# The copies of each pair's k, and the loads of a gain row, issued by GpSimd in an attention and gMLP kernel

## The chip, the core and the metric

One core of one Trainium2 chip runs the whole program. The metric is device time in microseconds of one execution. TensorE (PE) multiplies and transposes, VectorE (DVE) and ScalarE (ACT) do elementwise work, GpSimd (POOL) does a few memsets and copies, and SyncE (SP) issues most DMA transfers. Each engine takes its instructions in order. When an instruction must wait, all that stands behind it on the same engine waits too, and that holds for an engine that only issues DMAs.

## The reference

`x` is 512 by 1024 in float32. Two layers run one after the other, each with a mixer and a squared-ReLU MLP behind it. The first mixer is chunked attention with 16 heads of 64 columns, the second a gated MLP. Cut to the parts that matter here:

```python
def chunked_relpos_attention(h, w_in, q_gain, k_gain, rel_bias, w_out):
    q, k, v = jnp.split(h @ w_in, 3, axis=-1)
    q = rms_norm(q.reshape(B, S, A_HEADS, A_HEAD_DIM), q_gain) * (A_HEAD_DIM ** -0.5)
    k = rms_norm(k.reshape(B, S, A_HEADS, A_HEAD_DIM), k_gain)
    ...
        s = jnp.einsum('bihd,bjhd->bhij', qc, kb).astype(jnp.float32) + bias
        ...
        p = jax.nn.softmax(s, axis=-1).astype(vb.dtype)
        return jnp.einsum('bhij,bjhd->bihd', p, vb)
    ...
    return o @ w_out

def chunked_spatial_gating(h, w_in, v_gain, w_s, b_s, w_out):
    z = jax.nn.gelu(h @ w_in, approximate=False)
    u, v = jnp.split(z, 2, axis=-1)
    v = rms_norm(v, v_gain).reshape(B, nw, SG_WINDOW, SG_GROUPS, SG_HALF // SG_GROUPS)
    ...
    return (u * vm.reshape(B, S, SG_HALF)) @ w_out

def reference(x, c, ...):
    cond = jax.nn.silu(c)
    for i in range(DEPTH):
        mod = cond @ ada_w[i] + ada_b[i]
        sh1, sc1, g1, sh2, sc2, g2 = [t[:, None, :] for t in jnp.split(mod, 6, axis=-1)]
        h = rms_norm(x, norm_mix[i]) * (1.0 + sc1) + sh1
        ...
        x = x + g1 * y
        h = rms_norm(x, norm_ffn[i]) * (1.0 + sc2) + sh2
        x = x + g2 * squared_relu_mlp(h, ffn_w1[i], ffn_w2[i])
    return x
```

## The kernel before

Every product of two float32 matrices is made of parts in a shorter format: an operand is split into a rounded part ("hi") and what is left ("lo"), and products of the parts are added up in one bank of PSUM. So each weight block passes through three steps: a DMA loads it (L385 for blocks of k by 512 columns, L400 for the slabs of the attention's input weights), ACT casts it to hi (L388, L405), and DVE makes lo (L389, L406). SBUF is cut into 49 slots of 4 KB per partition (`SL`, tiles named `s`), PSUM into 8 banks (`PS`, tiles named `p`). A slot or bank is taken by the next tile that asks, and that tile's first writer waits for the last reader of the one before. A DMA into a used slot so waits for whoever read the old contents, copies by DMA among them.

The attention runs by pairs of heads, 0 to 7, in software-pipelined steps:

- `pair_a` (L1141) makes q and k of a pair from normed tokens: PE transposes them (L1149), q is split (L1153 on ACT, L1154 on DVE), and k is scaled and split into one buffer `kp`, hi by L1158 on ACT and lo by L1159 on DVE. Each head has 64 of the 128 partitions of `kp`. Eight DMA copies (L1163) per pair, SBUF to SBUF, 64 partitions by 512 columns (128 KB) each, put each head's k onto both halves of the partitions: hi into `ka`, lo into `kb`. With q hi on one half and q lo on the other, one matmul with `ka` and one with `kb` give all the products of a score block.
- `head_a` (L1171) loads a head's bias (L1177 on SP) and masks a corner of it (a memset on GpSimd, L1178).
- `head_b` (L1183) makes scores row block by row block: two matmuls (the helper's line, L92) with `ka` and then `kb`, bias and maximum on DVE (L1200), exp on ACT (L1205). Behind the second head of a pair, GpSimd widens the reciprocal row sums (L1210).
- `head_c` transposes the probabilities (L1238) and splits them (L1242 on ACT, L1243 on DVE). `head_d` multiplies them with v (L92), takes the result out of its bank (L1266 on ACT, L1267 on DVE), and scales by the row sums (L1273, L1275, L1282, L1283).

Between these steps stand fillers: the remaining projections of q, k and v (`filler`, with L400, L405, L406), reads of the conditioning weights (L179, L194), and towards the end the loads of the output weights `a_w_out` (`out_load`, L385) and of x again (L115).

In the gMLP, `u_block` (L1528) runs over six column blocks. Each loads a row of gains, spread over 128 partitions (`gain`, 256 KB, one buffer, L1531), which DVE uses at L1543. The gated half v was stored to DRAM by GpSimd before (L1410) and is read back by SP (L1415).

The order of instructions on every engine comes from a scheduler that works with its own estimates of durations, so an edit at one place can move instructions of other engines. SP's DMAs take turns on eight semaphores, GpSimd's on eight of their own; an issue waits for the DMA eight issues before it on the same ring.

Of the kernel before, what the change touches and what calls it, by code (L numbers as in the profile page):

```python
# [52 lines left out]
def trunk_kernel(  # L53
# [20 lines left out]
    V, A, G, T, SP = nc.vector, nc.scalar, nc.gpsimd, nc.tensor, nc.sync  # L74
# [10 lines left out]
    def f32(ap):  # L85
        return ap.bitcast(F32)

    def bank():
        return PS.get([P, 512], F32)
# [4 lines left out]
    def mm3(ps, lh, ll, rh, rl, start, stop, more=False):  # L94

        mm(ps, lh, rh, start, False, more)
        mm(ps, lh, rl, False, False, more)
        mm(ps, ll, rh, False, stop, more)
# [165 lines left out]
    def bg(n):  # L264

        for _ in range(min(n, len(bgl) + len(bgq) - keep[0])):
            while len(bgq) > keep[0] and len(bgl) <= lead[0]:
                load, use = bgq.popleft()
                load()
                bgl.append(use)  # L270
            with behind():
                bgl.popleft()()
# [12 lines left out]
    def new_actT(n):  # L285
        tiles, ids = [], []
        for _ in range(n // 2):
            h, i = SL.get([P, 2, 512], F32R)
            lo, j = SL.get([P, 2, 512], F32R)
            tiles.append((h, lo))  # L290
            ids.append((i, j))
        return tiles, ids
# [86 lines left out]
    def wload(src, nk, k0=0, engs=(V,)):  # L379
        n = src.shape[1]  # L380
        kp = 1024 // n
        w, ids = [], []
        for k in range(k0, k0 + nk, kp):
            raw, done = raw_tile([P, kp, n])
            loaded[0] = SP.dma_start(raw, src[k * P:(k + kp) * P, :].rearrange("(k p) n -> p k n", p=P))  # L385
            hi, i = SL.get([P, kp, n], F32R)
            lo, j = SL.get([P, kp, n], F32R)
            A.copy(hi, raw)  # L388
            engs[len(ids) // 2 % len(engs)].tensor_tensor(lo, raw, f32(hi), ALU.subtract)  # L389
            done()  # L390
            w += [(hi[:, o, :], lo[:, o, :]) for o in range(kp)]
            ids += [i, j]
        return w, ids
# [18 lines left out]
    def gemm_tok(actT, w, t, ps, k0=0, last=None, start=True, part=slice(None)):  # L412
        last = len(w) - 1 if last is None else last
        cols = slice(t * P, t * P + P)
        for k in range(len(w)):
            ah, al = actT[k0 + k]
            wh, wl = w[k][0][:, part], w[k][1][:, part]
            mm3(ps, ah[:, cols], al[:, cols], wh, wl, start and k0 + k == 0, k0 + k == last)
# [675 lines left out]
    def qk_tile(n, hf, t):  # L1094
        return qk[n, hf][t // 2][0][:, t % 2, :]

    def qk_free(n, hf):
        SL.free(*[i for _, i in qk[n, hf]])
# [42 lines left out]
    def pair_a(pr):  # L1141


        sl = slice(pr % 4 * P, pr % 4 * P + P)
        (q, i0), (ka, i1), (kb, i2), (kp, i3) = [SL.get([P, 2, 512], F32R) for _ in range(4)]
        for n in ("q", "k"):
            ps, pi = bank()
            for t in range(NT):
                T.transpose(ps[:, t * P:(t + 1) * P], qk_tile(n, pr // 4, t)[:, sl], ident)  # L1149
            if n == "q":  # L1150
                for e in range(2):
                    r, o = slice(e * 64, e * 64 + 64), slice(64 - e * 64, 128 - e * 64)
                    A.activation(q[r, e, :], ps[r, :], AF.Copy, scale=qkg[r, 0:1])  # L1153
                    V.scalar_tensor_tensor(  # L1154
                        q[o, e, :], ps[r, :], qkg[r, 0:1], f32(q[r, e, :]), ALU.mult, ALU.subtract
                    )
            else:
                A.activation(kp[:, 0, :], ps, AF.Copy, scale=qkg[:, 1:2])  # L1158
                V.scalar_tensor_tensor(kp[:, 1, :], ps, qkg[:, 1:2], f32(kp[:, 0, :]), ALU.mult, ALU.subtract)  # L1159
                for e in range(2):  # L1160
                    for o in (0, 64):
                        for part, dst in enumerate((ka, kb)):
                            SP.dma_start(f32(dst[o:o + 64, e, :]), f32(kp[e * 64:e * 64 + 64, part, :]))  # L1163
            PS.free(pi)
        if pr % 4 == 3:
            qk_free("q", pr // 4)
            qk_free("k", pr // 4)
        SL.free(i3)
        pairs[pr] = (q, ka, kb, (i0, i1, i2))

    def head_a(hd):  # L1171
        if hd % 2 == 0:
            pair_a(hd // 2)
        b = {}
        b["bias"], i = SL.get([P, 1024], F32)
        b["ids"] = [i]
        SP.dma_start(b["bias"][:, 0:512], a_rel[hd])  # L1177
        G.memset(b["bias"][0:64, 448:512], NEG)  # L1178
        hs[hd] = b
# [233 lines left out]
    def v_load(cb, b):  # L1413
        v, i = SL.get([P, 2, 512], F32)
        SP.dma_start(v.rearrange("p t n -> p (t n)"), vd[cb, b])  # L1415
        return v, i
# [111 lines left out]
    def u_block(cb):  # L1528
        w, ids = u_ahead.pop() if u_ahead else wload(b_w_in[0][:, cb * 512:(cb + 1) * 512], KD)
        gain = tp.tile([P, 512], F32, tag="gain", name="gain", bufs=1)  # L1530
        SP.dma_start(  # L1531
            gain, bass.AP(tensor=b_v_gain.tensor, offset=b_v_gain.offset + cb * 512, ap=[[0, P], [1, 512]])
        )
        vs_ = [v_load(cb, b) for b in range(2)]
        tiles, tids = new_actT(4)
        for t in range(NT):
            ps, pi = bank()
            gemm_tok(h, w, t, ps)
            uv, ui = SL.get([P, 2, 512], F32)
            u, vh = uv[:, 0, :], uv[:, 1, :]  # L1540
            A.activation(u, ps, AF.Gelu)
            PS.free(pi)
            V.scalar_tensor_tensor(vh, vs_[t // 2][0][:, t % 2, :], vr[:, t:t + 1], gain, ALU.mult, ALU.mult)  # L1543
            vs, vi = SL.get([P, 2, 512], F32R)
            A.copy(vs[:, 0, :], vh)
            V.tensor_tensor(vs[:, 1, :], vh, f32(vs[:, 0, :]), ALU.subtract)
            ps, pi = bank()
            c0 = 0
            parts = []
            while c0 < 512:  # L1550
                g = (cb * 512 + c0) // SGC
                c1 = min(512, (g + 1) * SGC - cb * 512)
                parts.append((g, c0, c1))
                c0 = c1
            for g, c0, c1 in parts:
                ws = wsT[g // 4][0][:, :, (g % 4) * P:(g % 4 + 1) * P]
                mm3(ps[:, c0:c1], ws[:, 0, :], ws[:, 1, :], vs[:, 0, c0:c1], vs[:, 1, c0:c1], True, True)
            for g, c0, c1 in parts:
                V.scalar_tensor_tensor(u[:, c0:c1], ps[:, c0:c1], bsT[:, g:g + 1], u[:, c0:c1], ALU.add, ALU.mult)
            PS.free(pi)  # L1560
            SL.free(vi)
            ps, pi = bank()
            for f in range(4):
                T.transpose(ps[:, f * P:(f + 1) * P], u[:, f * P:(f + 1) * P], ident)  # L1564
            cols = slice(t * P, t * P + P)
            for j in range(2):
                hi, lo = tiles[j]
                src = ps[:, j * 256:j * 256 + 256].rearrange("p (a b) -> p a b", a=2)
                A.copy(hi[:, :, cols], src)  # L1569
                V.tensor_tensor(lo[:, :, cols], src, f32(hi[:, :, cols]), ALU.subtract)  # L1570
            PS.free(pi)
            SL.free(ui)
            bg(1 if cb else 0)
            if (cb, t) == (5, 1):
                ahead[0] = wload(b_w_out[0][2048:3072, 0:512], KD)
        SL.free(*ids)
        SL.free(*[i for _, i in vs_])
        aTs[cb] = (tiles, tids)
# [5 lines left out]
    def b_down(blocks):  # L1584
# [16 lines left out]
        for b in blocks:  # L1601
            for i, j in aTs[b][1]:
                SL.free(i, j)

    u_block(0)
    u_block(1)
    b_down([0])
    u_block(2)
    b_down([1])
    u_block(3)  # L1610
# [55 lines left out]
```

## Time and profile before

| what | value |
|---|---|
| median of 3 runs (lowest to highest) | 1412.46 us (1410.62 to 1413.95) |
| the profiled execution | 1407.58 us, span 1405.8 us |
| mean granted clock of TensorE | 0.996 |
| ACT, DVE busy in the span | 711.3, 1021.7 us |
| copies of k (L1163) | 64, first 88.6 us, last 228.9 us |
| loads of `gain` (L1531) | 6, first 24.6 us, last 943.5 us |

In the profile L numbers are lines of the kernel. An arrow in brackets names what ended the idle time in front of an instruction. "SPq" is SP's issuing of DMAs, "DMA s<-in_a_w_out" a transfer itself from issue to landing, and a row of a timeline such as "x8" stands for eight instructions in a row. A row of a window gives its bounds, its length, the busy time of PE with its count of matmuls, the time of weight loads, DVE, ACT and GpSimd in the same manner, the granted clock, the busy share of the DMA engines, and the rate in GB/s.

### The profile page before, as it was taken

The page shows a single profiled execution, that of the slowest core. Times are in us where ns is not written, and L with a number is a line of the kernel's source. Part 1 is how long each engine was busy: PE and PEld are TensorE (multiplying, and loading weights), DVE is VectorE, ACT ScalarE, POOL GpSimd, SP SyncE. Part 2 cuts the span into 40 slices and gives each one's busy share as a digit, 9 for nine tenths or more (in the row PEclk, how much of TensorE's full clock was granted, in tenths as well). Part 3 has the DMA queues.
Part 4 walks back from the last instruction along what each step waited for, and adds up shares of the span by engine and source line. Part 5 has one row for each costly group of instructions (what it writes and reads, how often), then busy time and mean ns, then how long its engine had stood idle before and what let it go on. Part 6 is the DMA issues. An engine that isn't in the chain of part 4 may idle for free.

```text
span 1405.8 us, 18946 instructions
## 1 busy us (share of the span) xinstructions
PE 1383.6 (98%) x7226; PEld 1185.3 (84%) x7226; DVE 1021.7 (73%) x1494; ACT 711.3 (51%) x1229; POOL 15.7 (1%) x46
## 2 busy tenths in 40 slices
PE   9999998999999999999999999999999999999998
PEld 7899987789888888888888888888889988888887
DVE  7888998666667878777895746665677367766882
ACT  6547667555464544646586443223445455453630
POOL 0000000000000000000000000000000000000000
PEclk9999999999999999999999999999999999999999
DMA  9666566573253361456346535435437225242141
GB/s 374 242 172 206 162 174 195 179 270 106 75 195 119 123 222 60 138 192 240 135 157 236 184 100 176 151 127 165 142 113 270 76 90 180 71 140 90 31 165 60
DMA packets 85628, 221.53 MB, mean 158 GB/s; under 512 B 7960, under 2 KB 9376, under 8 KB 85536
## 3 DMA queue, kind: packets, MB, share of 16 engines
q1 hardware_dynamic: 83808, 214.01, 45.9%
q0 software_dynamic: 1728, 6.29, 1.1%
q8 instruction: 57, 0.93, 0.3%
q14 instruction: 35, 0.29, 0.1%
HBM read 197.21 MB, written 14.68 MB: 151 GB/s over the span
## 4 chain that ended last, share of the span: by engine, by line
PE 88%; DMA 5%; DVE 4%; ACT 2%; issue 1%; SPq 0%; DVEq 0%; ACTq 0%
PE p L92 86%; DMA s<-in_a_w_in 2%; DMA s<-in_ada_w 1%; PE p L1564 1%; DMA s<-in_a_w_out 1%; PE p L1238 1%; ACT s L483 1%; DVE s L1200 1%; PE p L315 1%; DVE s L1243 0%; DMA s<-in_b_w_in 0%; DVE s L955 0%; DMA s<-in_ffn_w 0%; DVE s L1267 0%; DVE s L1154 0%
## 5 line engine op out<-in xcount | busy, mean ns | idle before, releaser
L92 PE MATMUL p<-s,s 128*128 128x512 f32 (+2 forms) x6568 | 1322.6, 361 | 7.0 <-DVE nm L1200 2.0
L92 PEld LDWEIGHTS p<-s,s 128*128 128x128 f32 x6568 | 1109.5, 189 | 191.5 <-DVE nm L1200 3.0
L484 DVE TENSOR_TENSOR s<-s,s 128x1024 fp32r<-128x1024 f32 x234 | 280.0, 1220 | 115.5 <-ACT s L483 55.4
L483 ACT CAST s<-s 128x1024 fp32r<-128x1024 f32 x234 | 241.1, 1051 | 163.0 <-PE p L92 112.6
L389 DVE TENSOR_TENSOR s<-s,s 128x1024 fp32r<-128x1024 f32 x80 | 96.8, 1222 | 63.5 <-ACT s L388 51.1
L388 ACT CAST s<-s 128x1024 fp32r<-128x1024 f32 x80 | 83.5, 1051 | 92.6 <-DMA s<-in_b_w_in 36.2
L631 DVE TENSOR_TENSOR s<-s,s 128x1024 f32<-128x1024 f32 x64 | 77.6, 1220 | 32.0 <-DMA s<-in_ffn_w 31.6
L739 ACT ACTIVATE r<-p 128x512 f32<-128x512 f32 x64 | 38.1, 595 | 116.2 <-PE p L92 116.2
L194 DVE SCALAR_TENSOR_TENSOR s<-s,cs,s 128x1024 f32<-128x1024 f32 x70 | 89.6, 1280 | 5.7 <-DMA s<-in_ada_w 5.0
L517 DVE TENSOR_TENSOR s<-p,s 128x512 f32<-128x512 f32 x104 | 70.4, 685 | 19.1 <-PE p L92 17.9
L745 ACT ACTIVATE s<-r 128x256 f32<-128x256 f32 (+1 forms) x112 | 44.9, 443 | 1.2
L424 DVE TENSOR_TENSOR tr<-p,s 128x512 f32<-128x512 f32 (+1 forms) x33 | 22.0, 671 | 30.9 <-PE p L92 30.5
L1205 ACT ACTIVATE s<-s,nm 128x128 f32<-128x128 f32 (+3 forms) x64 | 36.0, 564 | 7.2 <-DVE nm L1200 5.6
L1200 DVE CUSTOM_DVE_ANT_0 s<-p,s 128x128 f32<-128x128 f32 (+3 forms) x64 | 29.7, 486 | 8.1 <-issue 4.7
L1569 ACT CAST s<-p 128x256 fp32r<-128x256 f32 x48 | 17.7, 370 | 34.9 <-PE p L1564 27.0
L530 DVE TENSOR_TENSOR s<-s,s 128x1024 f32<-128x1024 f32 x28 | 33.6, 1220 | 1.0 <-PE p L92 0.9
L1238 PE MATMUL p<-ident,s 128*128 128x128 f32 x160 | 25.0, 278 | 8.0 <-DVE s L1267 6.9
L304 ACT ACTIVATE s<-s 128x512 f32<-128x512 f32 x24 | 15.3, 638 | 33.9 <-DVE s L425 33.9
L1243 DVE TENSOR_TENSOR s<-p,s 128x512 fp32r<-128x512 f32 (+3 forms) x64 | 29.1, 485 | 3.7 <-ACT s L1242 3.3
L1570 DVE TENSOR_TENSOR s<-p,s 128x256 fp32r<-128x256 f32 x48 | 20.1, 418 | 15.4 <-ACT s L1569 15.4
L1242 ACT CAST s<-p 128x512 fp32r<-128x512 f32 (+3 forms) x64 | 24.9, 429 | 11.8 <-PE p L1238 11.4
L1543 DVE SCALAR_TENSOR_TENSOR s<-s,vr,gain 128x512 f32<-128x512 f32 x24 | 17.7, 748 | 16.8 <-PE p L92 11.7
(142 smaller groups left out, 755.5 us busy)
## 6 DMA issues: line engine op xcount, KB each, us to landing
s<-in_ffn_w SPq DMA_DIRECT2D x128, 512.0 KB, 4.6
s<-in_ada_w SPq DMA_DIRECT2D x96, 512.0 KB, 5.0
s<-in_b_w_in SPq DMA_DIRECT2D x48, 512.0 KB, 4.8
s<-in_b_w_out SPq DMA_DIRECT2D x24, 512.0 KB, 4.4
s<-in_a_w_in SPq DMA_DIRECT2D x22, 512.0 KB, 6.7
s<-s SPq DMA_DIRECT2D x64, 128.0 KB, 2.4
vd<-s POOLq DMA_DIRECT2D x12, 512.0 KB, 3.8
s<-vd SPq DMA_DIRECT2D x12, 512.0 KB, 3.6
```

What stands on the lines that cost most here:

```text
L92: T.matmul(ps, lhsT, rhs, start=start, stop=stop, skip_group_check=more)
L194: V.scalar_tensor_tensor(acc, r, ck, acc, ALU.mult, ALU.add)
L388: A.copy(hi, raw)
L389: engs[len(ids) // 2 % len(engs)].tensor_tensor(lo, raw, f32(hi), ALU.subtract)
L483: A.copy(self.hi, raw)
L484: mark[0] = V.tensor_tensor(self.lo, raw, f32(self.hi), ALU.subtract)
L517: V.tensor_tensor(dst, ps, dst, ALU.add)
L631: V.tensor_tensor(x[0], y_[0], z[0], ALU.subtract)
L739: A.activation(r, ps, AF.Relu)
L745: A.activation(d, v, AF.Square)
L1200: V.tensor_tensor_reduce(out=pt[it], in0=ps[:, 0:n], in1=b["bias"][:, 512 - n:512], scale=-1.0, scalar=-NEG, op0=ALU.add, op1=ALU.min, acc ...
L1238: T.transpose(ps[:, it * P:(it + 1) * P], b["pt"][it][:, jt * P:(jt + 1) * P], ident)
```

## The change

Two calls get another issuing engine, `G` (GpSimd) in place of `SP`: the eight copies of each pair, and the load of the gain row.

```diff
@@ -1160,7 +1160,7 @@
                 for e in range(2):
                     for o in (0, 64):
                         for part, dst in enumerate((ka, kb)):
-                            SP.dma_start(f32(dst[o:o + 64, e, :]), f32(kp[e * 64:e * 64 + 64, part, :]))
+                            G.dma_start(f32(dst[o:o + 64, e, :]), f32(kp[e * 64:e * 64 + 64, part, :]))
             PS.free(pi)
@@ -1528,7 +1528,7 @@
         gain = tp.tile([P, 512], F32, tag="gain", name="gain", bufs=1)
-        SP.dma_start(
+        G.dma_start(
             gain, bass.AP(tensor=b_v_gain.tensor, offset=b_v_gain.offset + cb * 512, ap=[[0, P], [1, 512]])
         )
```

The orders of PE, DVE and ACT differ only inside the attention, about 93 to 270 us of the profile of before.

SP, near the end of the attention (the piece of the difference; s_270, s_281 and s_299 are biases of heads, s_278 and s_279 are `ka` and `kb` of pair 7, s_284 to s_293 blocks of the first half of `a_w_out`):

```order
 L1177 DMA s_270_2797<-in_a_rel_bias 128x512
+L385 DMA s_284_2989<-in_a_w_out 128x2x512
 L385 DMA s_290_3001<-in_a_w_out 128x2x512
-L1163 DMA s_278_2908<-s_280_2910 64x512 x4
-L1163 DMA s_279_2909<-s_280_2910 64x512 x4
+L385 DMA s_287_2995<-in_a_w_out 128x2x512
 L1177 DMA s_281_2935<-in_a_rel_bias 128x512
-L385 DMA s_284_2989<-in_a_w_out 128x2x512
-L385 DMA s_287_2995<-in_a_w_out 128x2x512
-L385 DMA s_293_3007<-in_a_w_out 128x2x512
 L1177 DMA s_299_3057<-in_a_rel_bias 128x512
```

The loads of s_284 and s_287 now come ahead of the bias of s_281 with no copy in front of them; s_293, whose slot held pair 7's `kp`, has moved behind three loads of x.

ACT at the same place, before (s_285, s_291 and s_288 are the hi parts of `a_w_out` blocks; the L1266 is the one that reads p_183):

```order
L1242 CAST s_272_2865<-p_167_2868 128x512
L1205 ACTIVATE s_270_2797,sm<-s_270_2797,nm 128x256
L1205 ACTIVATE s_282_2963,sm<-s_282_2963,nm 128x384
L1225 CAST s_316_3306<-s_235_2406 128x2x2x64
L1205 ACTIVATE s_282_2963,sm<-s_282_2963,nm 128x512
L1315 COPY s_236_2407<-p_174_2938 128x2x256
L1242 CAST s_296_3013<-p_179_3016 128x512
L1225 CAST s_316_3306<-s_236_2407 128x2x2x64
L388 CAST s_285_2991<-s_284_2989 128x1024
L1205 ACTIVATE s_282_2963,sm<-s_282_2963,nm 128x128
L1266 COPY s_276_2895<-p_183_3038 64x512
```

And ACT there in the changed kernel:

```order
L1266 COPY s_276_2895<-p_171_2896 64x512
L388 CAST s_285_2991<-s_284_2989 128x1024
L388 CAST s_291_3003<-s_290_3001 128x1024
L1153 ACTIVATE s_277_2907<-p_172_2911,qkg 64x512
L388 CAST s_288_2997<-s_287_2995 128x1024
L1205 ACTIVATE s_270_2797,sm<-s_270_2797,nm 128x256
L1205 ACTIVATE s_282_2963,sm<-s_282_2963,nm 128x384
L1225 CAST s_316_3306<-s_235_2406 128x2x2x64
L1205 ACTIVATE s_282_2963,sm<-s_282_2963,nm 128x512
L1242 CAST s_296_3013<-p_179_3016 128x512
L1205 ACTIVATE s_282_2963,sm<-s_282_2963,nm 128x128
L1266 COPY s_276_2895<-p_183_3038 64x512
```

The cast into s_285 has moved from two places ahead of the L1266 of p_183 to ten ahead of it, with the casts into s_291 and s_288 close behind.

GpSimd around pairs 4 and 5 in the piece of the difference (s_202 and s_203 are `ka` and `kb` of pair 4, s_231 and s_232 those of pair 5; s_209 takes the widened row sums of pair 3; s_234 and s_243 are biases):

```order
 L1210 COPY s_209_2168<-rs 128x512
+L1163 DMA s_202_2054<-s_204_2056 64x512 x4
+L1163 DMA s_203_2055<-s_204_2056 64x512 x4
 L1178 MEMSET s_234_2403 64x64
+L1163 DMA s_231_2376<-s_233_2378 64x512 x4
 L1178 MEMSET s_243_2531 64x64
+L1163 DMA s_232_2377<-s_233_2378 64x512 x4
 L1210 COPY s_239_2485<-rs 128x512
```

Pair 4's copies stand behind the widening of pair 3's row sums, and pair 5's `kb` behind the corner of the bias s_243.

## The prediction

> **What bounds the kernel now.** I read the page first, for who is busy.
>
> ```profile
> span 1405.8 us, 18946 instructions
> PE 1383.6 (98%) x7226; PEld 1185.3 (84%) x7226; DVE 1021.7 (73%) x1494; ACT 711.3 (51%) x1229; POOL 15.7 (1%) x46
> ```
>
> TensorE (PE) works 1383.6 of 1405.8 us. All that an edit which leaves the arithmetic alone can win lies in the 22.2 us in which PE stands, and in stretches where its clock is lowered. POOL (GpSimd) is nearly unused, so it has room. Next I asked in which windows PE stands; the third column is its busy time, and the clock is the number ahead of the last two.
>
> ```profile
> 125.00:150.00 25.00, 22.50 (x176) 21.35 (x176) 22.93 (x53) 17.76 (x42) 0.90 (x3) 1.00 0.75 246
> 175.00:200.00 25.00, 21.56 (x152) 19.86 (x152) 22.51 (x59) 16.97 (x40) 1.21 (x4) 0.93 0.76 193
> 225.00:250.00 25.00, 20.74 (x124) 18.55 (x123) 16.97 (x37) 15.47 (x37) 0.90 (x3) 0.93 0.65 206
> 250.00:275.00 25.00, 21.59 (x113) 18.14 (x112) 17.39 (x34) 16.26 (x32) 0.61 (x1) 0.93 0.51 172
> 940.00:1020.00 80.00, 80.00 (x391) 67.26 (x391) 51.64 (x76) 30.18 (x45) 0.00 (x0) 1.00 0.50 161
> ```
>
> The attention stage is where time is lost: 2.50, 3.44, 4.26 and 3.41 us of idle PE in these four windows. The gMLP stage has none (80.00 of 80.00). Closer windows, and PE's own timeline, place the holes:
>
> ```profile
> 181.00:187.00 6.00, 3.86 (x12) 3.30 (x13) 6.00 (x19) 3.60 (x9) 0.00 (x0) 0.73 0.78 206
> 235.00:245.00 10.00, 6.43 (x26) 5.40 (x27) 8.78 (x19) 7.78 (x17) 0.76 (x2) 0.83 0.77 277
> 255.00:262.00 7.00, 3.72 (x13) 2.71 (x12) 5.74 (x10) 6.29 (x12) 0.61 (x1) 0.77 0.54 195
> ```
>
> ```profile
> 181.16 0.47 PE L92 MATMUL p<-s,s 128*128 128x256 f32 x2 [0.78 <-DVE s L1243]
> 183.61 5.25 PE L92 MATMUL p<-s,s 128*128 128x256 f32 x21 [1.98 <-ACT s L405]
> ...
> 224.13 3.93 PE L92 MATMUL p<-s,s 128*128 128x256 f32 x29
> ...
> 238.57 1.11 PE L1238 MATMUL p<-ident,s 128*128 128x128 f32 x4 [4.26 <-DVE s L1267]
> ...
> 242.85 8.27 PE L92 MATMUL p<-s,s 128*128 128x384 f32 x37
> ...
> 258.17 0.33 PE L1238 MATMUL p<-ident,s 128*128 128x128 f32 x1 [2.68 <-DVE s L1267]
> ```
>
> Three holes of about 2 us or more (1.98, 4.26, 2.68), and at each the granted clock falls: 0.73, 0.83 and 0.77 in those windows. A shortfall of (1 − 0.83) × 10.00 = 1.7 us at the second; 1.6 us each at the first and third. So each costs its idle time plus about 1.7 us.
>
> **Why PE stands at 238.57.** The chain of work back from there, then SP's (the sync engine's) issue timeline:
>
> ```profile
> 230.23 4.80 DMA s<-in_a_w_out
> 235.05 1.04 ACT s L388
> ...
> 236.52 0.58 ACT s L1266
> ...
> 237.84 0.69 DVE s L1267
> ...
> 251.30 3.76 DMA s<-in_a_w_out
> ```
>
> ```profile
> 219.78 0.39 SPq L385 DMA_DIRECT2D s<-in_a_w_out  x1
> 223.35 6.14 SPq L1163 DMA_DIRECT2D s<-s  x8
> 229.59 0.52 SPq L1177 DMA_DIRECT2D s<-in_a_rel_bias  x1
> 230.23 1.53 SPq L385 DMA_DIRECT2D s<-in_a_w_out  x3
> ```
>
> An out-projection weight block lands at 235.03. ACT, in order, casts it (L388) ahead of the copy L1266 that empties a bank, DVE adds (L1267), and PE may go on. That load was issued late, at 230.23, because SP stood at pair 7's eight copies: from 220.2 it waited for k, then took 6.14 us to issue them.
>
> **The change, part by part.** *Removed from SP*: 64 copies and what they wait for.
>
> ```profile
> L1163 SPq DMA_DIRECT2D s<-s x64: 461/595/1777, 88.6 to 228.9; - x64
> DMA to landing us min/median/max: 2.2/2.4/6.9
> ```
>
> ```profile
> SPq L1163 <- ACT s L1158: 19.9, 5, 7.6
> ```
>
> 64 × 0.595 = 38 us of issuing and 19.9 us of waiting leave SP. Only what was queued behind and was needed soon is worth anything. The Trainium skill, DMA: Bandwidth & Descriptors, section "Issuing engines are not separate DMA queues", says that starting DMAs on another engine saves only the sequencer's time to initiate them, usually small beside the transfer. By that alone the hole at 238.57 would stay, and the sum below would be +2.3 instead of −3.7; the chain above differs, since there 3.2 us of waiting and 6.14 us of issuing on SP, not a transfer, made the load late.
>
> *The hole at 238.57.* In the changed order on SP s_284, s_290 and s_287 come right behind the bias load of s_270, with no copy ahead, and the transposes that release s_284's buffer come 2.7 us of PE work earlier (I counted matmuls in order, at 3.93 / 29 = 0.135 us at most for 256 columns and 8.27 / 37 = 0.22 us for 512). So the three issue at about 221.3 to 223.3 in place of 230.2 to 231.8, and land by about 228.5. ACT's order has three casts (L388) right there, ahead of exps and of the L1266 that matters: 228.5 + 1.05 for the last cast, then about 3.2 us of exps, casts and copy, then L1267's 0.69: 233.9. PE wants it at 238.57 − 4.26 = 234.31. The hole closes with 0.4 us to spare: **−4.3, and −1.7 of clock: −6.0 us**.
>
> *The hole at 258.17* stays. Its load (251.30) waits for transposes of PE, not for SP. In the changed order a bank at the out-projection waits for that load, its cast, its residual and one L1243; about 4 us of PE work cover it, as now. **0**, from −3 (half closed, its clock loss gone) to +1 (the load now stands behind another one).
>
> *Added to POOL*: 64 issues, in order with its 16 memsets and 8 copies of row sums. What does an issue cost there?
>
> ```profile
> 174.69 0.61 POOL L1210 COPY s<-rs 128x512 f32<-128x512 f32 x1 [14.19 <-DVE rs L1206]
> ...
> 194.87 0.14 POOL L1178 MEMSET s<- 64x64 f32 x1 [14.17 <-DMA s<-in_a_rel_bias]
> ...
> 728.80 0.53 POOL L1410 DMA_DIRECT2D vd<-s  x1 [3.80 <-ACT s L1436]
> ```
>
> ```profile
> vd<-s POOLq DMA_DIRECT2D x12, 512.0 KB, 3.8
> ...
> xs<-s SPq DMA_DIRECT2D x8, 512.0 KB, 2.9
> ```
>
> POOL's own stores take 0.53 us each, but no two stand back to back, so the rate of eight in a row isn't shown. The same size lands 3.8 − 2.9 = 0.9 us later from POOL than from SP. Below: 0.53. Above: 0.53 + 0.9 = 1.4, if the 0.9 us is work that the next issue must wait for. I take 0.6, near the 0.53 and SP's 0.595, and a landing of 2.4 + 0.9 = 3.3 us.
>
> ACT's cast of k ahead of the copies:
>
> ```profile
> L1158 ACT ACTIVATE s<-p,qkg x8: 670/674/712, 87.9 to 222.7; 128x512 fp32r<-128x512 f32 x8
> ```
>
> The first matmul with kb needs six issues (four ka, two kb): k's transposes end, 0.7 us for L1158, six issues of u, 3.3 us to land: 4.0 + 6u, 7.6 us at u = 0.6. Against it stands PE's work between k's transposes and that matmul, counted in the new order: pair 0 7.3 us, pair 1 9.7, pair 4 5.0, pair 6 9.4, pair 7 11.2, the others over 15. So pair 0 loses 0.3 us, pairs 1, 6 and 7 nothing.
>
> *Pair 4* is the tight one. In POOL's order the row-sum copy of the pair before (174.69, done 175.30) now stands ahead of its copies, about 1.2 us after L1158 is done. And behind the copies hangs a chain that the hole at 183.61 already has:
>
> ```profile
> 175.30 2.48 DMA s<-s
> ...
> 177.85 4.64 DMA s<-in_a_w_in
> ...
> 182.51 1.05 ACT s L405
> ```
>
> The load of s_216 reuses k's buffer, so it waits for the last copy to land wherever that was issued. Now: kb late by 4.0 + 1.2 + 3.6 − 5.0 = 3.8 us; then the last two copies, the load and the cast (1.2 + 4.6 + 1.1 = 6.9) against 5.6 us of PE work: 1.3 us; clock 1.7. Before: 0.78 + 1.98 + 1.7 = 4.5. Net **+2.3 us**.
>
> *The gain loads*: each is 256 KB.
>
> ```profile
> gain<-in_b_v_gain SPq DMA_DIRECT2D x6, 256.0 KB, 5.3
> ```
>
> ```profile
> 20.00:40.00 20.00, 19.05 (x113) 16.40 (x113) 18.04 (x31) 10.56 (x16) 0.00 (x0) 1.00 1.03 406
> ```
>
> The first now goes out on POOL among its first memsets instead of inside a stretch in which the DMA engines are full (1.03 at 406 GB/s, so 0.65 us of it): −0.3, between −0.65 and 0. The other five lie where PE has no hole: 0, and a late one would cost its lateness.
>
> **Sum**: −6.0 + 0 + 0.3 + 2.3 − 0.3 = −3.7 us. The profiled execution took 1407.58 us (span 1405.8): 1403.9. That execution is 4.9 us under the median of 1412.46, so on the median's footing **1408.8 us**.
>
> **The rivals.** *Given back at the next wait.* The 0.4 us to spare at 238.57 is thin: loads that land 3 us later there, or pair 4 worse by 3 us, eat the gain: about 1411.8. For it: the three casts close together on ACT, and pair 5's kb, which in POOL's order stands behind the memset that ran at 194.87. Against: SP is free 8 us earlier, and with two issues and a landing that kb is there at 199.5; its first matmul comes 15.0 us of PE work and pair 4's 5 us of idle after k's transposes (ahead of 181.16 now, some 2 us later then), so at about 202.
>
> *It doesn't do what it says.* SP still waits for copies wherever a load reuses k's buffer (s_216, the bias of s_270, s_293), so the waiting may only move: then 1407.58 again, 1412.5 on the median. Against: s_284 and s_287 have no such wait.
>
> *Slower.* The mechanism is POOL's issue rate, at pairs 0, 1, 4 and 6. At u the terms are 6u − 3.3 (pair 0), 6u − 5.7 (pair 1), 8u + 0.3 − 2.8 (pair 4), 6u − 5.4 (pair 6). With −6.3 they come to zero at about u = 0.87. At 1.1: 3.3 + 0.9 + 6.3 + 1.2 − 6.3 = +5.4, so 1417.9. At 1.4 it would be +13, with pair 7 late too. For it: the 0.9 us of later landing must be spent somewhere. Against: each store occupied POOL for 0.53 us only. The Trainium skill, SBUF — State Buffer, in its box on the "DVE blocks DMA" trap, says that descriptors of DMAs issued from GpSimd can't be written while DVE runs an operation in a two-port fast mode. If each issue waited out one operation as long as L1267's 0.69 us (0.6 + 0.69 = 1.3), the formula with pair 7 gives +11, so 1423.7. The stores' 0.53 us beside a DVE that is 73% busy speaks against it; I give it 0.05 of this rival's 0.30.
>
> **How the numbers follow.** Forecast, with its neighbours down to u = 0.53: 0.45. Given back or not done as said: 0.25. POOL too slow: 0.30. About 0.2% (2.8 us) is what can be told from no change. The low end takes −3 at the hole of 258 and u = 0.53: 1403.5. The high end is u = 1.1: 1418; what lies beyond, and under the low end, is some 2 in 10. Faster 0.46, same 0.25, slower 0.29.
>
> **What would show it.** Right: the a_w_out loads issue at about 221 to 224, no idle of over 1 us near 234 to 239, clock 1.00 there; POOL's copies 0.6 us apart; 2 to 4 us idle at pair 4 near 178 to 190; the hole before the second half's weights still near 3 us. Wrong: copies 0.9 us apart or more, with idle ahead of the first scores of pairs 0, 1 and 6; an L1267 still ending a 4 us wait; a gain load that DVE's L1543 waits for.

## The result, and the profile after

The changed kernel is slower: **1426.12 us** (median of 4 runs, 1425.46 to 1426.73) beside 1411.54 us for the kernel before on the same chip, a ratio of **1.0105 [1.0083, 1.0127]**. The forecast was 1408.8, so the miss is 17.3 us, and the time lies 8 us beyond the range's end. The profiled execution took 1425.46 us, with a mean granted clock of 0.987 in place of 0.996.

The head of the page after:

```profile
span 1423.6 us, 19012 instructions
PE 1392.8 (98%) x7226; PEld 1192.8 (84%) x7226; DVE 1023.3 (72%) x1494; ACT 710.5 (50%) x1229; POOL 51.7 (4%) x116
```

TensorE has the same 7226 matmuls. It is idle for 30.8 us instead of 22.2, and the matmuls take 9.2 us more, which goes with the lower clock. The windows say where. Columns as before: bounds, length, PE, weight loads, DVE, ACT, GpSimd, clock, DMA share, GB/s. The first row of each kernel holds pairs 0 and 1 and the loads around them. The second and third of after are shifted by about 17 us, so that they hold about the work of the second and third of before.

Before:

```profile
90.00:125.00 35.00, 35.00 (x276) 33.59 (x276) 30.96 (x69) 23.87 (x60) 1.04 (x4) 1.00 0.77 207
158.00:208.00 50.00, 45.88 (x342) 43.27 (x343) 46.99 (x131) 33.35 (x82) 1.81 (x6) 0.97 0.59 158
232.00:248.00 16.00, 11.74 (x59) 10.04 (x57) 11.16 (x25) 10.32 (x24) 0.90 (x3) 0.89 0.69 244
```

After:

```profile
90.00:125.00 35.00, 27.76 (x197) 25.85 (x196) 24.32 (x48) 16.70 (x39) 8.99 (x18) 0.85 0.49 130
175.00:225.00 50.00, 44.22 (x317) 40.54 (x318) 44.92 (x126) 29.89 (x73) 10.01 (x22) 0.93 0.54 158
249.00:265.00 16.00, 13.02 (x69) 10.90 (x68) 11.25 (x23) 10.33 (x26) 0.96 (x3) 0.89 0.67 195
...
940.00:1020.00 80.00, 80.00 (x380) 66.78 (x378) 48.13 (x70) 24.32 (x37) 0.54 (x1) 1.00 0.41 134
```

In the first window PE stood nowhere before (35.00 of 35.00 at 1.00). Now it is idle for 7.24 us, at a clock of 0.85, which is another 0.15 × 35 = 5.25 us of clock at most. By the trace the clock is at half from 103.67 to 113.91, and PE is idle for 4.3 of these 10.24 us, so about 3 us of lost clock are left: **some 10 us at pairs 0 and 1**. (A clock share worked out from a window below is an upper figure in the same way.) The gMLP stage has no idle time now either (80.00 of 80.00).

Matmuls at the same place in PE's order show the lag directly: after is 4.9 us late at pair 0's first transpose (the 426th, 85.06 against 80.13), 15.5 us late at the 640th, behind the holes at pair 0 (122.35 against 106.81), and 17.8 us late at the end of the span. So in these two traces 4.9 us came at the start, 10.6 at pairs 0 and 1, and all the rest adds 2.3.

What GpSimd issues now, by the copies' line, and PE's waits:

```profile
L1163 POOL DMA_DIRECT2D s<-s x64: 516/523/536, 93.8 to 247.7; - x64
...
DMA to landing us min/median/max: 2.2/4.4/8.4
```

```profile
PE p L92 <- DMA s<-s: 5.9, 5, 1.9
...
PE p L1238 <- DVE s L1267: 1.8, 1, 1.8
```

Before, the list had this instead:

```profile
PE p L1238 <- DVE s L1267: 6.9, 2, 4.3
```

An issue costs 0.523 us, with 0.536 at most, so the rate that the "slower" rival feared is at its best end. But a copy lands 4.4 us after its issue, not 2.4, and up to 8.4. A wait of PE for copies, absent from the waits of before, now takes 5.9 us. The waits for L1267 have shrunk from 6.9 to 1.8 us: those at 238.57 and 258.17 are gone, and the one that is left stands at another place, behind the first scores of pair 4 (206.30 in after).

PE's timeline at pair 0:

```profile
100.17 0.76 PE L92 MATMUL p<-s,s 128*128 128x256 f32 x3 [1.07 <-DMA s<-s]
102.84 0.88 PE L92 MATMUL p<-s,s 128*128 128x128 f32 x4 [1.91 <-DMA s<-s]
104.60 1.33 PE L92 MATMUL p<-s,s 128*128 128x256 f32 x3 [0.88 <-DMA s<-s]
109.31 2.93 PE L92 MATMUL p<-s,s 128*128 128x256 f32 x12 [3.39 <-DVE nm L1200]
```

And the chain of work back from the last of these:

```profile
97.81 8.84 DMA s<-in_a_w_in
...
106.75 1.05 ACT s L405
...
107.82 0.07 DVE s L406
...
108.97 0.28 DVE s L1200
```

Three holes (3.86 us together) wait for copies. The fourth (3.39 us) waits for DVE's L1200, and that stands in DVE's order behind the subtraction L406 of a filler's weights, which took 8.84 us to land and then had to be cast. These four are all the idle time of that window; the copies of pair 1 made PE wait nowhere. SP's issue timeline, after and then before, says what stood beside them:

```profile
96.50 1.64 SPq L400 DMA_DIRECT2D s<-in_a_w_in  x2
```

```profile
88.59 5.29 SPq L1163 DMA_DIRECT2D s<-s  x8
...
94.61 0.40 SPq L400 DMA_DIRECT2D s<-in_a_w_in  x1
95.11 5.32 SPq L1163 DMA_DIRECT2D s<-s  x8
100.52 0.53 SPq L400 DMA_DIRECT2D s<-in_a_w_in  x1
```

Before, SP could send the first of the two 512 KB loads (s_128, s_131) only once all of pair 0's copies were issued, and the second only behind pair 1's. Freed of the copies, SP sends both at 96.50 to 98.14, while pair 0's copies (93.80 to 98.02) are still on their way. By the trace, from issue to landing:

```
                         before        after
pair 0's eight copies    2.2 to 2.4    2.2, 2.9, 3.4, 4.7, 5.0, 6.2, 6.5, 7.1
the two loads            4.7, 4.8      7.4, 8.8
pair 1's eight copies    3.8 to 4.7    5.0 to 7.1
```

### The profile page after: what moved, and what is told of

It reads as the page before. It is cut to its first block, busy times and chain, and to the rows that moved or that the text cites. A ratio compares the mean times of both kernels' runs of the same rounds, so it can differ in the third digit from the quotient of the medians.

```text
span 1423.6 us, 19012 instructions
## 1 busy us (share of the span) xinstructions
PE 1392.8 (98%) x7226; PEld 1192.8 (84%) x7226; DVE 1023.3 (72%) x1494; ACT 710.5 (50%) x1229; POOL 51.7 (4%) x116
## 4 chain that ended last, share of the span: by engine, by line
PE 88%; DMA 5%; DVE 4%; ACT 1%; issue 1%; POOL 0%; SPq 0%; DVEq 0%; ACTq 0%
PE p L92 86%; DMA s<-in_ada_w 3%; DMA s<-in_a_w_in 1%; PE p L1564 1%; PE p L1238 1%; PE p L315 1%; DVE s L955 0%; DVE s L194 0%; DVE s L1243 0%; ACT s L1205 0%; DMA s<-in_ffn_w 0%; DMA s<-s 0%; DVE s L1200 0%; PE p L1149 0%; DMA s<-in_a_w_out 0%
## 5 line engine op out<-in xcount | busy, mean ns | idle before, releaser
L517 DVE TENSOR_TENSOR s<-p,s 128x512 f32<-128x512 f32 x104 | 70.5, 686 | 19.0 <-PE p L92 17.8
L1163 POOL DMA_DIRECT2D s<-s x64 | 32.7, 521 | 32.7 <-ACT s L1158 21.9
L1243 DVE TENSOR_TENSOR s<-p,s 128x512 fp32r<-128x512 f32 (+3 forms) x64 | 29.2, 486 | 4.5 <-ACT s L1242 4.3
L1200 DVE CUSTOM_DVE_ANT_0 s<-p,s 128x128 f32<-128x128 f32 (+3 forms) x64 | 28.9, 485 | 3.7 <-PE p L92 3.6
```

The costliest lines, as they stand in the source:

```text
L517: V.tensor_tensor(dst, ps, dst, ALU.add)
```

## The experiments

The question was why the copies land late. In the expectations, theory C is **sharing**: SP's loads, sent earlier, run beside the copies in the same transfer engines, whoever issues the copies. Theory D is a cost of **GpSimd's own**: its descriptors come late, or wait while DVE works. Ratios are against the kernel before, run on the same chip.

**The two edits apart.** First the copies alone:

```diff
-    SP.dma_start(f32(dst[o:o + 64, e, :]), f32(kp[e * 64:e * 64 + 64, part, :]))
+    G.dma_start(f32(dst[o:o + 64, e, :]), f32(kp[e * 64:e * 64 + 64, part, :]))
```

> Only the copies of k go to GpSimd, the gain loads stay on SP; PE, ACT and DVE get the changed kernel's order unchanged. Theory G (the first gain load, issued by GpSimd at the very start, costs some 4.8 us by 27 us into the trace, 1.7 of it in the landing of x and the rest in half-clock stretches): about 4 to 6 us less than the changed kernel, some 1421, with no half-clock stretch before 90 us; the loss at pairs 0 and 1 (some 11 us) stays. Rival (the late start is the noise of one execution, or comes from the new order): as the changed kernel, 1426.

1423.31 us (1421.21 to 1425.49), 1.0102 [1.0078, 1.0125]. The window of pairs 0 and 1 with the copies alone:

```profile
90.00:125.00 35.00, 29.13 (x199) 26.78 (x198) 23.17 (x50) 17.84 (x43) 9.27 (x19) 0.85 0.57 160
```

5.87 us of idle time and at most 0.15 × 35 = 5.25 of clock: up to 11.1 us, against nothing before. By place in PE's order (the 426th to the 640th matmul) it is 9.8. What was expected of the start did not come: the ratio is the changed kernel's (1.0102 against 1.0105), so by the ratio taking the gain loads out won next to nothing, and the clock was at half from 17.90 to 24.73 us all the same. Then the gain loads alone:

```diff
-        SP.dma_start(
+        G.dma_start(
             gain, bass.AP(tensor=b_v_gain.tensor, ...
```

> Only the gain loads go to GpSimd; PE, ACT and DVE keep the order of the kernel before. Theory G: 3 to 5 us slower than the kernel before, x landing 1.5 to 2 us later than its 8.70, half-clock stretches between 10 and 30 us. Rival (the start loss needs the copies' order): within 1 us of before.

1412.90 us (1410.95 to 1417.88), 1.0024 [1.0010, 1.0038]: about 3.4 us slower. GpSimd's issue of the first gain load, from its timeline:

```profile
1.50 0.67 POOL L1531 DMA_DIRECT2D gain<-in_b_v_gain  x1
```

It goes out at 1.50, among the loads of x at the very start, the one place where PE has nothing to do until a load lands. By the trace the last of the first four blocks of x lands at 10.43 us instead of 8.70. Together 1.0102 and 1.0024 would make 1.0126, at the upper end of the changed kernel's interval (1.0083 to 1.0127). So the copies make most of the loss; what the gain loads add on top of them lies between nothing and the 3.4 us that they cost alone.

**The gain loads, first one late.**

```diff
+        with tc.issue_after(widened[0].ins): G.dma_start(
```

(`widened[0]` is the last L1210, so the first load stands behind the attention's work in GpSimd's order.)

> Only the gain loads go to GpSimd, and the first is held until behind the last row-sum copy (about 258 us); every other engine keeps the order of before. Theory (the gain loads cost only by the place of the first one, inside the first loads of x): within 1 us of before, x landing at 8.7 us. Rival (loads of gain from GpSimd cost wherever they are): 3 us slower, as with all of them moved.

1411.46 us, 1.0000 [0.9986, 1.0014], with x landed at 8.81. The other five gain loads cost nothing from GpSimd; all of the loss is the first one's place.

**Another queue for the copies: ACT's.**

```diff
-    SP.dma_start(f32(dst[o:o + 64, e, :]), f32(kp[e * 64:e * 64 + 64, part, :]))
+    A.dma_start(f32(dst[o:o + 64, e, :]), f32(kp[e * 64:e * 64 + 64, part, :]))
```

> The copies are issued by ACT's queue, gain loads stay on SP: SP is free of the copies as in the changed kernel, but the descriptors aren't written by GpSimd. Theory D (a DMA from GpSimd reaches the transfer engines late and unevenly): copies land 2.2 to 2.6 us after issue as SP's do, the first matmul with kb of pair 0 does not wait 1.9 us, and the loss at pairs 0 and 1 is gone; about 1408 to 1414, if ACT's 64 issues of some 0.5 us delay its exps little. Rival C (the copies land late because SP, freed, sends loads beside them): landing as late as from GpSimd (4.4 us median), loss of some 10 us at pairs 0 and 1.

1432.48 us, 1.0168 [1.0144, 1.0191], outside what was expected. PE's wait for copies, and the copies' line:

```profile
PE p L92 <- DMA s<-s: 15.3, 5, 5.3
```

```profile
L1163 ACTq DMA_DIRECT2D s<-s x64: 468/608/785, 90.7 to 254.4; - x64
...
  ACT s L1315: 11.0, 3
...
DMA to landing us min/median/max: 2.2/2.4/7.3
```

By the trace pair 0's first copies land after 2.2 to 2.5 us, and the rest after 4.5 to 7.3, from when SP's loads join at 93.6. So the lateness at pair 0 comes without GpSimd too. The median over all 64 copies, 2.4 us, is what theory D expected, though: where no load runs beside them, as at pair 1, these copies land after 2.2 to 2.4 us. The excess over the copies-alone run has two candidates: eight issues of 0.6 us stand in front of ACT's own work (L1315 waited 11.0 us for them), and 9.3 us of PE's wait for copies lie at pair 7. This run can't separate them, so the next one measures sharing by itself.

**The transfers by themselves.** A kernel that leaves out the whole computation and runs groups of eight copies between barriers: from SP (`a`), from GpSimd (`b`), two 512 KB loads (`l`), SP's copies beside two loads (`c`), GpSimd's beside two loads (`d`), GpSimd's beside eight DVE operations of two kinds (`e`, `f`), SP's beside DVE (`g`).

```diff
+    copies(G, "d")
+    loads(SP, "d", 2)
+    cut()
+    copies(G, "e")
+    stt(8)
```

> Leaves out the whole computation; sections apart by barriers, each with the eight 128 KB copies of one pair: from SP alone, from GpSimd alone, then each with two 512 KB weight loads issued on another queue at the same time, then from GpSimd beside eight DVE operations like L194 and beside eight like L406, and from SP beside L194's kind; two loads alone as well. Theory C (copies and loads share the transfer engines, and the loads that SP may now send beside the copies make both late): alone, all copies land 2.2 to 3.1 us after issue from either queue, the last of eight at about 6 to 7 us; beside two loads the last lands 3 to 5 us later from either queue, and the loads at 7 to 9 us in place of about 4; DVE changes nothing. Theory D (GpSimd's DMAs are late by themselves or held up by DVE): from GpSimd alone the eighth lands over 2 us later than from SP, or beside DVE's operations each copy is some 0.7 to 1.3 us later.

From its list of DMA issues (count, KB each, median us to landing):

```profile
lw<-in_a_w_in ACTq DMA_DIRECT2D x2, 512.0 KB, 3.7
...
dw<-in_a_w_in SPq DMA_DIRECT2D x2, 512.0 KB, 5.1
...
akb<-kp SPq DMA_DIRECT2D x4, 128.0 KB, 2.3
...
bkb<-kp POOLq DMA_DIRECT2D x4, 128.0 KB, 3.2
...
ckb<-kp SPq DMA_DIRECT2D x4, 128.0 KB, 6.2
...
dkb<-kp POOLq DMA_DIRECT2D x4, 128.0 KB, 6.7
...
ekb<-kp POOLq DMA_DIRECT2D x4, 128.0 KB, 3.1
...
fkb<-kp POOLq DMA_DIRECT2D x4, 128.0 KB, 3.1
```

By the trace, from the first issue to the eighth landing it took 6.72 us from SP alone, 6.76 from GpSimd alone, 10.25 and 10.3 beside two loads, and 6.57 and 6.56 from GpSimd beside DVE. Two loads add 3.5 us whoever issues the copies, and DVE adds nothing. The loads themselves slowed less than expected: 4.2 to 6.0 us beside the copies, where 7 to 9 was forecast, and 3.3 and 4.1 alone. Each figure is from one execution. Theory C holds here; D falls for these operations, except that a copy from GpSimd lands some 0.9 us later by the median (3.2 against 2.3), which its faster issuing makes good by the eighth.

**Pairs 0 and 1 left on SP.**

```diff
+    (SP if pr < 2 else G).dma_start(f32(dst[o:o + 64, e, :]), ...
```

> The copies of pairs 0 and 1 stay on SP, those of pairs 2 to 7 go to GpSimd, gain loads on SP. Theory (some 10 to 11 us of the loss arise at pairs 0 and 1, the rest of the attention about pays for itself): 1411 to 1414. Rival (each pair loses a little, so the loss goes with their number): three quarters of the 13 us, about 1420.

1413.21 us (1410.11 to 1417.43), 1.0017 [1.0004, 1.0030]. The window of pairs 0 and 1 is whole again:

```profile
90.00:125.00 35.00, 35.00 (x277) 33.67 (x276) 31.09 (x66) 22.55 (x55) 5.75 (x12) 1.00 0.74 209
```

So some 12 of the 14 us that the copies cost (1.0102 against 1.0017; by the two intervals, 8 to 16) go with two of the eight pairs.

**The two loads put behind the copies.** Copies on GpSimd as in the first run, and the loads of one filler block (s_128, s_131) on GpSimd too, where they stand behind pair 0's copies:

```diff
-            loaded[0] = SP.dma_start(
+            loaded[0] = q.dma_start(
...
+    wload_slabs(a_w_in, D * (1280 + i * 256), 2, 256, q=G if (n, cb) == ("k", 2) else SP)
```

> The copies on GpSimd as in the run with the copies alone, and with them the two loads of one filler block (s_128 and s_131, 512 KB each), issued by GpSimd too, so that in GpSimd's order they stand behind the copies of pair 0, about where SP's order had them before. PE's order differs a little from that run in the scores of pair 0. Sharing theory (the copies land late because SP, now free, sends these loads beside them): pair 0's copies land 2.2 to 4.5 us after issue, the 4 to 6 us of idle and the half clock at pair 0 go, and the time falls from 1423 to 1411 to 1417. Pair 1's copies, behind the loads, stay late. If the copies are late because GpSimd issues them, whatever SP sends: they land as late as before this edit, and the time stays at 1420 to 1425.

1416.46 us (1414.08 to 1423.37), 1.0042 [1.0025, 1.0060]. Two windows, of pairs 0 and 1 and of what follows:

```profile
90.00:125.00 35.00, 34.12 (x270) 32.57 (x269) 30.08 (x59) 21.76 (x50) 10.67 (x23) 1.00 0.64 178
...
125.00:150.00 25.00, 20.71 (x146) 19.45 (x145) 19.82 (x44) 15.30 (x38) 5.68 (x13) 0.86 0.70 203
```

Pair 0's copies, issued by GpSimd at the same rate, now land after 2.3 to 4.3 us (by the trace), and the window loses 0.9 us instead of up to 11.1. Pair 1's, behind the loads, stay late (4.0 to 6.7 us), as expected. That is the sharing theory's forecast, by an edit that leaves the copies as they were. Only about 8.5 us of it arrive at the end (1.0102 against 1.0042): the next window, with pair 2, loses 4.3 us idle and up to 0.14 × 25 = 3.5 of clock here, where it lost 2.8 and 1.3 with the copies alone. There too a load of SP (126.72) runs beside the copies, which land after up to 7.5 us.

**All filler loads behind or among the copies.** The same with `q=G` for every filler block.

> All loads of the filler blocks (L400 inside the attention) go out on GpSimd together with the copies, so that one queue holds both in one order again, as SP's did before; only the loads of the output weights and the biases stay on SP. If what was lost is only the common order of copies and loads: the waits at pairs 0 to 2 go and the time comes to 1409 to 1414, with 1.5 us or more perhaps left at pair 7, which these loads don't touch. If copies from GpSimd cost something by themselves that the run with two loads moved did not undo: 1416 or more.

1421.54 us (1415.50 to 1423.15), 1.0076 [1.0057, 1.0095]: a miss. The profile, of the fastest of its runs, has almost no wait for copies left:

```profile
PE p L92 <- DVE nm L1200: 5.8, 4, 3.1
PE p L1149 <- DVE nm L1200: 3.5, 1, 3.5
...
PE p L92 <- DMA s<-s: 1.1, 2, 0.9
```

The waits for copies are 1.1 us in place of the changed kernel's 5.9, but others of DVE took their place: the orders of the engines differ here from the kernel before, and loads on GpSimd now stand behind its waits for k. One common queue is then not enough to win the time back; which of those two makes these waits is not shown.

**Pair 7 alone: the gain that was forecast.**

```diff
+    (G if pr == 7 else SP).dma_start(f32(dst[o:o + 64, e, :]), ...
```

> Only pair 7's eight copies go to GpSimd; the order is the kernel before's up to about 218 us. Theory (the hole of 4.26 us at 238.57 comes from a_w_out's loads behind these eight issues on SP): loads issue at 221 to 225, the hole and its half-clock stretch go, 4 to 6 us faster than before, some 1406. Rival (the loads land no earlier, or pair 7's own copies land 4 to 8 us late and make PE wait for kb): within 2 us of before.

1411.05 us (1409.00 to 1413.78), 1.0011 [1.0001, 1.0020]. PE's timeline there:

```profile
235.98 0.30 PE L92 MATMUL p<-s,s 128*128 128x128 f32 x1 [1.12 <-DMA s<-s]
237.45 0.90 PE L1238 MATMUL p<-ident,s 128*128 128x128 f32 x3 [1.17 <-ACT s L1315]
...
274.48 10.83 PE L92 MATMUL p<-s,s 128*128 128x512 f32 x39 [2.49 <-ACT s L1282]
```

The hole of 4.26 us is gone, and 1.12 for pair 7's own copies (which land after 4 to 8 us beside the earlier a_w_out loads), 1.17 behind it, and a new 2.49 at the last pair's output stand in its place. The expected gain didn't come.

**The other way round: a_w_out's loads on GpSimd, copies on SP.**

```diff
-            loaded[0] = SP.dma_start(raw, ...
+            loaded[0] = q.dma_start(raw, ...
...
+    wload(a_w_out[0][:, hf * 512:hf * 512 + 512], KD, q=G)
```

> Copies and gain loads as in the kernel before; instead the eight loads of a_w_out are issued by GpSimd. They no longer stand behind pair 7's copies on SP. Theory (the hole of 4.26 us at 238.57 is a matter of the loads' place in SP's order): the first three loads are issued by 225, the hole goes with its half-clock stretch, 3 to 6 us faster than before. Rival (loads that go beside pair 7's copies make these late, and PE waits for kb instead): within 2 us of before, with PE waiting for copies near 232 to 238.

1411.49 us, 1.0008 [0.9995, 1.0022]. PE's timeline, of the slowest of its runs (1415.93):

```profile
239.98 0.45 PE L92 MATMUL p<-s,s 128*128 128x128 f32 x1 [2.85 <-DMA s<-s]
...
280.50 5.06 PE L92 MATMUL p<-s,s 128*128 128x512 f32 x11 [3.25 <-ACT s L1282]
```

The first three loads go out at 223.65, 227.80 and 228.54, the first ahead of pair 7's copies and the other two among them. SP's first two copies land after about 4 us, and from the third on they take 7 to 10.7. In both runs, whichever queue holds which, pair 7's copies are late beside these loads.

**A version a little faster than before.** The other link of the prediction's chains is the load of s_216, which waits for copies because it takes `kp`'s slot. Here the slot is given back at the end of the pair's scores instead; all DMAs stay on SP:

```diff
-        SL.free(i3)
-        pairs[pr] = (q, ka, kb, (i0, i1, i2))
+        pairs[pr] = (q, ka, kb, (i0, i1, i2, i3))
```

> Copies and gain loads on SP as in the kernel before. One other edit: the slot of kp is given back two steps later (at the end of the pair's scores) instead of straight behind its copies, so that no load takes that slot and waits for the copies; loads such as s_216 find another slot. It aims at the hole at 183.61 (1.98 us and 1.6 us of clock). If that wait goes and nothing takes its place: 1407 to 1409 beside 1410.6. If the load then waits for another slot's reader, or the wait ends at the next link as in the two runs that moved the hole of 238.57: 1410 to 1413. The slots are scarce, so a load that finds none in time could also make it 1414 or more.

1406.33 us (1404.22 to 1413.46, 5 runs), 0.9971 [0.9947, 0.9995]. The same kernel again, with more rounds:

> The kernel with only the later return of kp's slot, once more with more rounds, since its first interval ends close to 1 (0.9947 to 0.9995). A real gain: a ratio of 0.995 to 0.9985 with the interval below 1. Chance: an interval that holds 1.

1408.33 us (1404.62 to 1410.58, 12 runs) beside 1409.57, 0.9982 [0.9970, 0.9994]. Its PE timeline in the first of the two runs, where holes above 1 us are left between 175 and 262 us:

```profile
180.46 0.69 PE L1238 MATMUL p<-ident,s 128*128 128x128 f32 x2 [2.85 <-DVE s L1159]
...
237.70 1.75 PE L1238 MATMUL p<-ident,s 128*128 128x128 f32 x7 [2.51 <-ACT s L1315]
```

Two holes of 2.85 and 2.51 us where there were three of 1.98, 4.26 and 2.68: a small gain, by 0.2 to 0.3%, near the limit of what can be told, and clear of 1 in both intervals. But it isn't the gain that was aimed at. The wait for the weights' cast (L405) did go, and PE waits 2.85 us for DVE's L1159 there instead:

```profile
175.00:200.00 25.00, 21.05 (x143) 18.82 (x142) 23.50 (x65) 14.90 (x36) 1.89 (x4) 0.86 0.72 185
```

That window is idle for 3.95 us at 0.86, where it was 3.44 at 0.93 before. The time came back elsewhere, most plainly where the hole of 258.17 was: from 250 to 275 us PE is idle for 1.73 us at 1.00, where it was 3.41 at 0.93. The expectation did not name that hole, and why it closed isn't shown.

## Why the prediction was wrong, point by point

**The step that failed** is the price of the copies at pairs 0 and 1: "4.0 + 6u, 7.6 us at u = 0.6", with "a landing of 2.4 + 0.9 = 3.3 us", and so "pair 0 loses 0.3 us, pairs 1, 6 and 7 nothing". The 3.3 us came from transfers in the old order. The prediction saw that SP is freed and used this for a_w_out, but not here: SP, no longer held up by the copies, sends two 512 KB loads into the time in which the copies run. With u = 0.523, copies that took 2.2 to 7.1 us to land at pair 0, and loads that took 7.4 and 8.8, pairs 0 and 1 cost 10.6 us where 0.3 was forecast. All the idle time of it is at pair 0: 3.86 us behind the copies, and 3.39 behind the late weights, a wait that the sum did not have. The run with pairs 0 and 1 left on SP and the one with the two loads put behind the copies show place and mechanism. The transfers by themselves show the size: two loads add 3.5 us to eight copies, and in the kernel pair 0's eight took 10.76 us from first issue to last landing, 7.05 before.

**The issue rate** was right in direction: 0.523 us is under the 0.6 taken, and the "slower" rival's mechanism (over 0.87 us) did not occur. The side it stood for did, by another mechanism that the prediction had not named.

**The start** was forecast at −0.3, and the gain loads alone cost about +3.4 (1.0024). The reading "now goes out on POOL among its first memsets instead of inside a stretch in which the DMA engines are full" missed that PE waits for the loads of x there, and 256 KB more beside them made the fourth block land 1.7 us later. The two profiles differ by 4.9 us at pair 0, but part of this is chance: in the eleven traces with the old start pair 0 begins anywhere from 80.13 to 84.13, with 0 to 10.24 us at half clock ahead of it, and in the two with the early gain load at 85.06 and 86.72. The profile of before is the earliest of all.

**The hole at 238.57** was forecast at −6.0. The mechanism is right: a_w_out's loads go out at 240.67 to 243.2 in after's time, about 223.5 to 226 in before's (221.3 to 223.3 was forecast), and the wait for L1267 there is gone. The size is wrong by what it gave back. In the aligned window idle time fell only from 4.26 to 2.98 us (16.00 − 11.74 and 16.00 − 13.02), with the clock at 0.89 in both. Pair 7's copies, up to 8.4 us in landing beside those same loads, opened waits of 0.67 and 1.39 us in after's PE timeline:

```profile
253.01 0.30 PE L92 MATMUL p<-s,s 128*128 128x128 f32 x1 [0.67 <-DMA s<-s]
255.05 0.89 PE L92 MATMUL p<-s,s 128*128 128x128 f32 x3 [1.39 <-DMA s<-s]
```

This is the rival "given back at the next wait", though the waits are for late copies, which it had not named. The runs with pair 7 alone and a_w_out's loads on GpSimd show it by themselves. "Pairs 1, 6 and 7 nothing" so held for pair 1 but not for pair 7. The hole at 258.17 was forecast to stay, and in size it did: 248 to 285 us of before has 3.41 us of idle time and 265 to 302 of after 3.00, both at a clock of 0.95, though PE waits for L1243 there now.

**Pair 4** was forecast at +2.3. Its aligned window loses 5.78 us idle and up to 0.07 × 50 = 3.5 of clock, where it lost 4.12 and 0.03 × 50 = 1.5: at most +3.7, of the right sign and about the size. The mechanism is another, so that is partly luck. None of PE's five waits for copies lies at pair 4, and the row-sum copy was done at 189.55, ahead of L1158's end at 190.41, so it held nothing up. PE's longer waits there are for DVE:

```profile
197.14 5.84 PE L92 MATMUL p<-s,s 128*128 128x512 f32 x17 [2.29 <-DVE s L1243]
...
206.30 0.66 PE L1238 MATMUL p<-ident,s 128*128 128x128 f32 x4 [1.77 <-DVE s L1267]
```

**Sharing, and DVE.** The Trainium skill, DMA: Bandwidth & Descriptors, section "Issuing engines are not separate DMA queues", says that DMAs from different issuing engines run on the same DMA engines and interleave, so that another issuing engine saves only the time to initiate. The runs agree on the sharing, and it mattered more than the weight it had: copies and loads from two engines slowed one another (10.25 and 10.3 us in place of 6.72 and 6.76). What the prediction took from it, that the hole at 238.57 would stay, did not come: its wait for L1267 is gone. The Trainium skill, SBUF — State Buffer, in its box on the "DVE blocks DMA" trap, says that GpSimd can't write descriptors while DVE runs an operation in a two-port mode. Eight copies from GpSimd took 6.57 and 6.56 us beside two kinds of DVE operation, and 6.76 without, so no run here shows such a delay; whether those two operations run in that mode isn't shown either.

**What stays open.** Of after's loss at pairs 0 and 1, the idle time divides into 3.86 us behind late copies and 3.39 behind the late filler weights; how much of the lost clock belongs to each isn't separated. How much the early gain load costs on top of the moved copies lies between nothing and 3.4 us. In the run with all filler loads on GpSimd, the cause of the new waits isn't settled.

## What to carry to other kernels

An in-order DMA queue is also a brake: moving some transfers off it lets what stood behind them start earlier, so for every DMA moved, list the loads that are set free and ask which transfers PE waits for will then run beside them. Take a landing time from a row in which the new neighbours run too, not from the old order. And a load that is not needed for long stays out of the first microseconds, whoever issues it.

## What the hardware showed

- Eight 128 KB SBUF-to-SBUF copies take the same time from SP and from GpSimd (6.72 and 6.76 us to the last landing). GpSimd issues one every 0.51 us back to back, SP one every 0.63; what GpSimd gains there it gives back in the landing (medians over the eight of 3.1 to 3.2 us against 2.3). The 0.9 us that the prediction took from GpSimd's stores is about that size, and the next issue did not wait for it.
- Lost clock went with idle time, and cost less than the window's mean says: by after's trace four holes of 0.88 to 3.39 us (7.25 together) go with 10.24 us at half clock, but PE was idle in 4.3 of these, so some 3 us of work were lost. Before, single holes of 1.98, 4.26 and 2.68 us each go with 3.41 us at half clock, and three of 0.70 to 0.96 us between 133 and 146 us with none.
- Runs of the kernel that puts the two loads behind the copies differ by 9 us (1414.08 to 1423.37), with mean clocks from 0.994 down to 0.988. What sets the clock apart from run to run isn't shown.
